# A SwiGLU feed-forward in split fp32 on one core: per-set pairs with an interleaved down projection, against shared weights and a down phase of its own

## Chip, cores and metric

One core of one Trainium2 chip. The metric is the device time of one execution of the whole kernel in microseconds (us); the median of three runs stands for a kernel. The profile of one further execution shows where the time goes. Engines: PE is TensorE's matmul unit (PEld its weight load), DVE is VectorE, ACT is ScalarE, POOL is GpSimd, SP is SyncE, which here issues the DMAs.

## What is computed

One layer of an encoder for T = 1088 tokens (1024 prompt and 64 sample tokens), width 1024, inner width 2816. The part at issue comes last: the output projection of the mixing branches, a norm, and the gated feed-forward.

```python
x = x + mixed @ w_out
h = rmsnorm(x, g_ffn)
return x + (jax.nn.silu(h @ w_gate) * (h @ w_up)) @ w_down
```

## The kernel before

All tensors are float32, and TensorE is given each operand as a rounded high part and a remainder: a product of two blocks is three matmuls, high by high, high by low, low by high (`matmul3`, L115). A high part is made by a copy with rounding (ACT, or POOL in `round_hi`, L91), a remainder by a subtraction on DVE (`lo_of`, L85). "Preparing" a block below means these two steps. Weights come in blocks of 512 KB through a ring of three tiles `raw` (or two tiles `fr`) in SBUF; `wblock` (L102) loads and prepares one.

Activations lie with the channels on the partitions and the tokens along the free axis. The tokens are two sets, `SETS`: set 0 is columns 0 to 511, set 1 columns 512 to 1087 (576 columns).

`y` (from L960) holds the residual stream in SBUF from here to the end. `out_proj(i)` (L1005) adds `mixed @ w_out` for set i, block row f by block row f, and sums the squares; `norm_stat` and `norm_rows` turn these into `rb`, a row of norm factors on all partitions. `block_sums(i, rb)` (L1053) multiplies the norm in and forms, for the four channel blocks k, the seven block combinations of the activations that a product by seven multiplications of 2x2 blocks needs, each with its high part (`hi`) and remainder (`lo`). For set 0 it runs inside `out_proj(1)`, whose matmuls cover it. For set 1 its 28 combinations are called at one place, between the last pair of set 0 and the first of set 1 (L1193).

The feed-forward (driver from L1176) goes over sets, and in a set over 11 pairs p of inner blocks. `hidden(p, i)` (L1137) makes gate and up, each by `pair_product` (L1092): seven products of a weight combination (`ws`, four or five of them by an add on POOL or DVE, prepared into `ah` and `al`) with the activation combinations, 12 matmuls each of 256 columns (set 0) or 288 (set 1). The results leave PSUM one by one, four by ACT copies to `st`, and are put together by adds on POOL and DVE. So each weight combination is made and prepared twice, once per set: 2 x 11 x 14 = 308 times. The hidden values u = silu(gate) * up stay in SBUF, prepared.

`down(p, us, i)` (L1156) is cut into eight units (one for each block row of the output), which are put between the products of the next pair: six matmuls and a DVE add of the result to `y` (L1170), 264 adds in all. After the last pair each finished block of `y` goes out at once (L1172).

What sets the order: the program is written as above, a scheduler then gives each engine one fixed order; an instruction waits for its data, for a free buffer of its ring, and for everything ahead of it on its engine. SP issues all DMAs in such an order too, so that a DMA that waits holds those behind it.

## Time and profile before

| | us |
|---|---|
| runs, median (lowest to highest) | 1814.99 (1814.76 to 1815.98) |
| the profiled execution | 1814.24 |
| its span | 1812.5 |
| PE busy | 1745.9 (96%), 12066 matmuls |
| DVE busy | 1437.3 (79%), 2767 instructions |
| ACT busy | 842.1 (46%) |
| POOL busy | 832.7 (46%) |
| DMA moved | 198.25 MB, mean 109 GB/s, fullest fortieth of the span 256 GB/s |
| chain of waits that ended last: share of PE | 60% |

The time of a run is the span and some 1.7 us around it. "Busy" counts an instruction from its start to its modelled end, and matmuls overlap, so that a busy PE still has its pace: what a matmul costs is the distance from its start to the next one's. The granted clock says how fast TensorE was allowed to run; at half of it every matmul takes twice as long.

### The profile page before, as it was taken

The numbers are of one execution on the slowest core, as the hardware profiler recorded it, in microseconds if no ns is written. First come the engines' busy times: TensorE is split into PE (matmuls) and PEld (weight loads), VectorE is DVE, ScalarE is ACT, GpSimd is POOL, SyncE is SP. The second block draws the span as 40 slices with busy tenths as digits, with TensorE's granted clock in tenths as the row PEclk, the third lists the DMA queues.
The fourth block names the chain that finished last, engine by engine and source line by source line (L and its number), as shares of the span: only waits on it lengthen the run. The fifth ranks groups of instructions, "written<-read, shape, count | busy, mean of one in ns | idle before, by whom it ended". The sixth has DMA issues, their size and how long they took to land.

```text
span 1812.5 us, 32877 instructions
## 1 busy us (share of the span) xinstructions
PE 1745.9 (96%) x12066; PEld 1679.2 (93%) x12066; DVE 1437.3 (79%) x2767; ACT 842.1 (46%) x1977; POOL 832.7 (46%) x885
## 2 busy tenths in 40 slices
PE   6999999999999998999999899999997899999999
PEld 6999999899999997899998889899996799999999
DVE  6657999998853436877664899899899999898896
ACT  4456677736423443477422443444443434344442
POOL 4102323343531125876014666566657665555543
PEclk9999999999999998999999999999998899999999
DMA  7223431134365327620543223232232232222322
GB/s 226 64 66 94 160 119 57 65 114 129 105 182 150 99 91 256 199 81 12 223 133 93 82 82 105 84 123 86 96 103 82 99 111 93 83 92 84 105 76 71
DMA packets 123598, 198.25 MB, mean 109 GB/s; under 512 B 21031, under 2 KB 91807, under 8 KB 123438
## 3 DMA queue, kind: packets, MB, share of 16 engines
q1 hardware_dynamic: 123438, 196.16, 33.8%
q8 instruction: 95, 1.56, 0.4%
q14 instruction: 65, 0.53, 0.1%
HBM read 158.47 MB, written 37.65 MB: 108 GB/s over the span
## 4 chain that ended last, share of the span: by engine, by line
PE 60%; DVE 6%; POOL 4%; issue 2%; ACT 1%; DMA 1%; SPq 0%; DVEq 0%; ACTq 0%; POOLq 0%
PE mm L120 46%; PE fl L120 8%; PE acc L927 2%; DVE lo L86 1%; PE tr L892 1%; PE mm L916 1%; DVE al L86 1%; DMA side_a<-gt 1%; POOL sm L901 1%; POOL pr L902 1%; DVE wlo L86 1%; DVE ws L1109 0%; POOL ws L1109 0%; PE mm L600 0%; ACT pr L900 0%
## 5 line engine op out<-in xcount | busy, mean ns | idle before, releaser
L120 PE MATMUL mm<-hi,ah 128*128 128x256 f32 (+1 forms) x1232 | 357.8, 291 | 9.7 <-ACT hi L1080 6.1
L120 PE MATMUL mm<-hi,al 128*128 128x256 f32 (+1 forms) x1232 | 357.6, 291 | 7.7 <-DVE al L86 7.7
L120 PE MATMUL mm<-lo,ah 128*128 128x256 f32 (+1 forms) x1232 | 358.4, 291 | 5.6 <-DVE lo L86 5.6
L86 DVE TENSOR_TENSOR al<-ws,ah 128x512 fp32r<-128x512 f32 x220 | 218.3, 1004 | 54.6 <-ACT ah L1114 52.2
L120 PE MATMUL mm<-u,whi 128*128 128x288 f32 (+1 forms) x1056 | 258.2, 330 | 0.7 <-DVE u L86 0.7
L1114 ACT CAST ah<-ws 128x512 fp32r<-128x512 f32 x220 | 135.4, 619 | 248.9 <-POOL ws L1109 141.9
L120 PEld LDWEIGHTS mm<-hi,ah 128*128 128x128 f32 x1232 | 234.4, 190 | 17.0 <-ACT hi L1080 8.3
L120 PEld LDWEIGHTS mm<-lo,ah 128*128 128x128 f32 x1232 | 234.1, 190 | 11.3 <-DVE lo L86 6.9
L120 PEld LDWEIGHTS mm<-hi,al 128*128 128x128 f32 x1232 | 233.3, 190 | 12.0 <-DVE al L86 11.3
L120 PE MATMUL fl<-hh,whi 128*128 128x362 f32 (+1 forms) x576 | 189.7, 330 | 0.7 <-ACT hh L133 0.7
L120 PE MATMUL fl<-hl,whi 128*128 128x362 f32 (+1 forms) x576 | 190.3, 331 | 0.0
L120 PE MATMUL fl<-hh,wlo 128*128 128x362 f32 (+1 forms) x576 | 189.3, 329 | 0.0
L120 PEld LDWEIGHTS mm<-u,whi 128*128 128x128 f32 x1056 | 175.1, 189 | 9.3 <-DVE u L86 1.1
L120 PE MATMUL mm<-u,wlo 128*128 128x288 f32 (+1 forms) x528 | 174.0, 330 | 0.0
L1109 POOL TENSOR_TENSOR ws<-raw 128x512 f32<-128x512 f32 x66 | 88.5, 1353 | 116.7 <-DVE al L86 116.7
L1170 DVE TENSOR_TENSOR y<-mm,y 128x288 f32<-128x288 f32 (+1 forms) x264 | 134.6, 523 | 7.4 <-PE mm L120 7.4
L96 POOL TENSOR_SCALAR whi<-raw 128x1024 fp32r<-128x1024 f32 x44 | 55.2, 1255 | 182.1 <-PE mm L120 168.4
L120 PE MATMUL mm<-tmhi,hh 128*128 128x256 f32 (+3 forms) x432 | 122.8, 289 | 1.2 <-POOL tmhi L96 1.1
L120 PE MATMUL mm<-tmlo,hh 128*128 128x256 f32 (+3 forms) x432 | 122.3, 285 | 0.7 <-DVE tmlo L86 0.7
L120 PE MATMUL mm<-tmhi,hl 128*128 128x256 f32 (+3 forms) x432 | 122.2, 285 | 0.0
L762 ACT ACTIVATE junk_a<-score,cand_a,sgn_a 128x512 f16<-128x512 f32 (+2 forms) x93 | 95.5, 1027 | 46.4 <-DVE cand_a L779 22.7
L86 DVE TENSOR_TENSOR wlo<-raw,whi 128x1024 fp32r<-128x1024 f32 x76 | 103.6, 1363 | 13.1 <-ACT whi L94 7.1
(369 smaller groups left out, 4865.4 us busy)
## 6 DMA issues: line engine op xcount, KB each, us to landing
raw<-in_w_up_dram SPq DMA_DIRECT2D x44, 512.0 KB, 4.1
fr<-in_w_gate_dram SPq DMA_DIRECT2D x44, 512.0 KB, 4.4
raw<-in_w_down_dram SPq DMA_DIRECT2D x44, 512.0 KB, 4.6
fraw<-in_w_gates_dram SPq DMA_DIRECT2D x24, 512.0 KB, 3.8
side<-side_a SPq DMA_DIRECT2D x8, 1088.0 KB, 6.9
raw<-in_w_out_dram SPq DMA_DIRECT2D x16, 512.0 KB, 3.6
gt<-side_m SPq DMA_DIRECT2D x16, 384.0 KB, 4.6
raw<-in_w_om_dram SPq DMA_DIRECT2D x12, 512.0 KB, 4.4
```

The costliest lines, as they stand in the source:

```text
L86: V.tensor_tensor(lo, src, hi.bitcast(F32), op=OP.subtract)
L96: G.tensor_scalar(hi, src, 1.0, 1.0, op0=OP.mult, op1=OP.mult)
L120: PE.matmul(ps, l, r, start=i == 0, stop=i == n - 1)
L762: A.activation(junk[:n, :nk], sc, AF.Sign, bias=bj, scale=1.0 if scale is None else scale[:n, j:j + 1], accum_out=sj)
L892: PE.matmul(lg[:n, i * 512:i * 512 + cn], qT[:, h, :n], kT[:, kv, s, k0 + c:k0 + c + cn], start=s == 0, stop=s == 1)
L901: G.tensor_tensor(sm, sm, mone[:n], op=OP.pow)
L902: G.tensor_scalar(pr, pr, sm, 0.5, op0=OP.mult, op1=OP.mult)
L916: PE.transpose(pt[:cn, i * n:(i + 1) * n], probs[i][:, c:c + cn], ident[:n, :n])
L927: PE.matmul(acc, l, r[:, es], start=ji == 0 and par == 0 and i == 0, stop=ji == nj - 1 and par == 1 and i == 2)
L1109: (V if m in (0, 5) else G).tensor_tensor(t, w, part(*z), op=op)
L1114: A.copy(wf, w)
L1170: V.tensor_tensor(y[:, f, c0:c0 + cn], ps, y[:, f, c0:c0 + cn], op=OP.add)
```

## The change

`y` is split in two tiles, one for each set, and `out_proj` also writes each finished block to DRAM (`y_d`), so that both tiles are given up once the norms are in. The seven products are put in another form, in which results that are summed share a PSUM bank: `chain` takes four products, `side` two, `one` one, and three intermediate sums leave by ACT copies while DVE makes three adds (before: four copies, POOL adds and four DVE adds). Of the four weight combinations three are made on DVE and one on POOL.

The first three pairs (`EARLY`) run for set 0 alone. The combinations of set 1 (`second_sums`, the new `block_sums(1, k, ...)` in four pieces) are called after pair 0 (piece 0), pair 1 (pieces 1 and 2) and pair 2 (piece 3). Pairs 0 to 2 follow for set 1, and pairs 3 to 10 for both sets with one preparation of the weights: 196 in place of 308. u is not prepared but stored to DRAM (`u_d`).

Down is a phase of its own. For each of three column chunks (364, 362, 362 columns, `CH`) the whole result, 8 blocks, stands in the 8 PSUM banks, while 22 inner blocks kb go by: u is loaded back (`uf`) and prepared (`uh`, `ul`), a weight block of 512 KB is loaded and prepared, 24 matmuls follow. At a chunk's end each block is added to its part of `y_d` (ring `yt` of three tiles) and stored. The host lays `w_down` out by kb, and the loads become 66 of rows of 4 KB (before 44). `round_hi` uses ACT alone from the first pair on (`third[0] = 2`).

```diff
-        if turn[0] % 2 and third[0]:
+        if third[0] and (turn[0] % 2 or third[0] > 1):
             A.copy(hi, src)
...
+ys = [None, yp.tile([128, KT, SETS[1][1]], F32, name="y1")]
+y_d = dram.tile([KT, 128, T], F32, name="y_d")
...
-                V.tensor_tensor(y[:, f, c0:c1], ps, y[:, f, c0:c1], op=OP.add)
+                V.tensor_tensor(y[:, f, d0:d1], ps, y[:, f, d0:d1], op=OP.add)
+                SP.dma_start(y_d[f, :, c0:c1], y[:, f, d0:d1])
...
+    def block_sums(i, k, rb, H, sums):
...
+        for e in range(2):
+            kk = k + 4 * e
+            V.scalar_tensor_tensor(hb[e][:, :n], ys[i][:, kk], gffn_c[:, kk:kk + 1], rb[:, :n], op0=OP.mult, op1=OP.mult)
+        b11, b12, b21, b22 = hb[0][:, :h], hb[0][:, h:n], hb[1][:, :h], hb[1][:, h:n]
+        t1, t2, t3, t4 = [t[:, :h] for t in sums]
+        for q, x, z, op, y_ in ((0, b11, None, None, None), (4, t1, b12, OP.subtract, b11), (2, b22, None, None, None),
+                                (5, t2, b22, OP.subtract, t1), (6, t3, b22, OP.subtract, b12),
+                                (1, b21, None, None, None), (3, t4, b21, OP.subtract, t2)):
+            if op:
+                (G if q == 6 else V).tensor_tensor(x, z, y_, op=op)
+            A.copy(H[0][q][:, k], x)
+            lo_of(H[1][q][:, k], x, H[0][q][:, k])
...
+        def product(dst, w, q, start, stop, then):
+            if turn2[0] % 2 == 0:
+                pair_w[:] = split_tiles()
...
+            A.copy(wh, w)
+            lo_of(wlo, w, wh)
...
+            for i in sets:
+                j = 0
+                for k in range(4):
+                    x, z = HH[i][0][q][:, k], HH[i][1][q][:, k]
+                    for l, r in ((wh[:, k], x), (wh[:, k], z), (wlo[:, k], x)):
+                        PE.matmul(dst[i], l, r, start=start and j == 0, stop=stop and j == 11, skip_group_check=True)
+                        j += 1
+                then(i)
...
+        product(chain, a11, 0, True, False, lambda i: A.copy(t11[i], chain[i]))
+        s1 = wsum(V, a21, OP.add, a22)
+        product(side, s1, 4, True, False, lambda i: A.copy(t22[i], side[i]))
+        s2 = wsum(V, s1, OP.subtract, a11)
+        product(chain, s2, 5, False, False, lambda i: A.copy(t12[i], chain[i]))
+        s4 = wsum(V, a12, OP.subtract, s2)
+        product(side, s4, 2, False, True, add(t12, side))
+        s3 = wsum(G, a11, OP.subtract, a21)
+        product(chain, s3, 6, False, False, add(t22, chain))
+        product(one, a12, 1, True, True, add(t11, one))
+        product(chain, a22, 3, False, True, lambda i: finish(i, t21[i], chain[i]))
...
+            SP.dma_start(u_d[p][0, :, t0:t0 + n], gi[:, 0].rearrange("p c t -> p (c t)"))
...
+    EARLY = 3
+    for p in range(EARLY):
+        hidden(p, (0,), True)
+        if p == 0:
+            rb = norm_rows(1, *st.pop())
+        for k in ((0,), (1, 2), (3,))[p]:
+            second_sums(k, rb)
...
+    for p in range(EARLY):
+        hidden(p, (1,))
+    for p in range(EARLY, NP):
+        hidden(p, (0, 1))
...
+    for c0, cn in CH:
+        acc = [mm()[:, :cn] for f in range(KT)]
+        for kb in range(NF):
+            p, e = kb // 2, kb % 2
+            uf = dn.tile([128, 364], F32, name="uf", tag="uf", bufs=2)[:, :cn]
+            SP.dma_start(uf, u_d[p][e, :, c0:c0 + cn])
+            wh, wlo = wblock(a["w_down"][kb], (KT, 128))
+            uh, ul = [dn.tile([128, 364], F32R, name=nm, tag=nm, bufs=2)[:, :cn] for nm in ("uh", "ul")]
+            A.copy(uh, uf)
+            lo_of(ul, uf, uh)
+            for f in range(KT):
+                for j, (l, r) in enumerate(((wh[:, f], uh), (wh[:, f], ul), (wlo[:, f], uh))):
+                    PE.matmul(acc[f], l, r, start=kb == 0 and j == 0, stop=kb == NF - 1 and j == 2)
+        for f in range(KT):
+            yt = dn.tile([128, 364], F32, name="yt", tag="yt", bufs=3)[:, :cn]
+            SP.dma_start(yt, y_d[f, :, c0:c0 + cn])
+            V.tensor_tensor(yt, acc[f], yt, op=OP.add)
+            SP.dma_start(o[0][f, :, c0:c0 + cn], yt)
```

How the order moves, at three places (each row: line of its kernel, operation, output, inputs, shape; numbers tell buffers apart).

**The combinations of set 1 on DVE.** Before, at the turn from set 0 to set 1 (`tg` from L1070 are the normed channels, `lo` the remainders of the combinations):

```order
L1070 SCALAR_TENSOR_TENSOR tg_16726<-y_11018,gffn_c_336,rb_13648 128x576 x2
L86 TENSOR_TENSOR lo5_16678<-st_16704,hi5_16671 128x288
L1070 SCALAR_TENSOR_TENSOR tg_16749<-y_11018,gffn_c_336,rb_13648 128x576 x2
L1170 TENSOR_TENSOR y_11018<-mm_16886,y_11018 128x512
L86 TENSOR_TENSOR lo0_16673<-tg_16726,hi0_16666 128x288
L1078 TENSOR_TENSOR st_16727<-tg_16726 128x288
L86 TENSOR_TENSOR lo1_16674<-tg_16726,hi1_16667 128x288
L86 TENSOR_TENSOR lo2_16675<-st_16727,hi2_16668 128x288
L86 TENSOR_TENSOR lo0_16673<-tg_16749,hi0_16666 128x288
L1078 TENSOR_TENSOR st_16750<-tg_16749 128x288
```
Now, after pair 0 of set 0 (`fr` from L1073 are the normed channels; `wlo` and `ws` are the weights of pair 1, `tg0` its results):

```order
L1073 SCALAR_TENSOR_TENSOR fr_13230<-y1_11018,gffn_c_336,rb_12911 128x576
L1097 TENSOR_TENSOR ws_13098<-raw_13078 128x512
L86 TENSOR_TENSOR wlo_13057<-raw_12947,whi_13056 128x512
L1128 TENSOR_TENSOR tg0_12944<-mm_12950,tg0_12944 128x256
L86 TENSOR_TENSOR wlo_13057<-raw_13076,whi_13056 128x512
L1080 TENSOR_TENSOR st_13206<-fr_13208,st_13206 128x288
L86 TENSOR_TENSOR lo4_12643<-st_13206,hi4_12636 128x288
L86 TENSOR_TENSOR lo6_12645<-st_13206,hi6_12638 128x288
L86 TENSOR_TENSOR lo5_12644<-st_13206,hi5_12637 128x288
L86 TENSOR_TENSOR lo0_12639<-fr_13230,hi0_12632 128x288
L1097 TENSOR_TENSOR ws_13117<-ws_13098,raw_13076 128x512
L86 TENSOR_TENSOR wlo_13101<-ws_13098,whi_13100 128x512
```
The work has moved from the turn between the two sets to a place among the weights and the results of set 0's early pairs. All four pieces stand between the results of pair 0 and the end of pair 2's gate in DVE's order.

**SP at the end of a chunk.** Before, at the kernel's end:

```order
L1097 DMA raw_21373<-in_w_up_dram 128x1024
L1097 DMA raw_21375<-in_w_up_dram 128x1024
L110 DMA raw_21452<-in_w_down_dram 128x4x256
L110 DMA raw_21613<-in_w_down_dram 128x4x256
L110 DMA raw_21691<-in_w_down_dram 128x4x256
L1172 DMA out_0_dram<-y_11018 128x288 x16
```
Now, from the last weight loads of the first chunk into the second (`raw` and `uf` belong to the second chunk, `yt` and `out` to the first):

```order
L1222 DMA uf_18871<-u0_11645 128x362
L110 DMA raw_18945<-in_w_down_dram 128x1024
L1222 DMA uf_18907<-u1_11646 128x362
L1234 DMA out_0_dram<-yt_18795 128x364
L1234 DMA out_0_dram<-yt_18799 128x364
L1234 DMA out_0_dram<-yt_18803 128x364
L1232 DMA yt_18807<-y_d_11019 128x364
L110 DMA raw_18981<-in_w_down_dram 128x1024
L1232 DMA yt_18811<-y_d_11019 128x364
L1232 DMA yt_18815<-y_d_11019 128x364
L1222 DMA uf_18943<-u1_11646 128x362
```
The finished blocks now share SP's order with the next chunk's loads, and from the fourth block on a `yt` load stands behind the store that frees its tile.

**PE at the same place.** Before, units of the last pair (one PSUM tile for each block row):

```order
L120 MATMUL mm_21733<-u_21557,whi_21692 128x288 x2
L120 MATMUL mm_21733<-u_21557,wlo_21693 128x288
L120 MATMUL mm_21733<-u_21561,whi_21692 128x288 x2
L120 MATMUL mm_21733<-u_21561,wlo_21693 128x288
L120 MATMUL mm_21742<-u_21557,whi_21692 128x288 x2
```
Now, the first blocks kb of the second chunk (`mm_18827` to `mm_18834` are its eight banks; `uh_18843` is kb 0, `uh_18879` kb 1):

```order
L1229 MATMUL mm_18827<-uh_18879,wlo_18875 128x362
L1229 MATMUL mm_18828<-ul_18880,whi_18874 128x362
L1229 MATMUL mm_18828<-uh_18879,wlo_18875 128x362
L1229 MATMUL mm_18829<-ul_18880,whi_18874 128x362
L1229 MATMUL mm_18829<-uh_18879,wlo_18875 128x362
L1229 MATMUL mm_18830<-uh_18843,whi_18838 128x362
L1229 MATMUL mm_18830<-ul_18844,whi_18838 128x362
L1229 MATMUL mm_18830<-uh_18843,wlo_18839 128x362
L1229 MATMUL mm_18830<-uh_18879,whi_18874 128x362
L1229 MATMUL mm_18830<-ul_18880,whi_18874 128x362
L1229 MATMUL mm_18830<-uh_18879,wlo_18875 128x362
L1229 MATMUL mm_18831<-uh_18843,whi_18838 128x362
```
The first two blocks kb go through three banks, then both through the fourth bank, both through the fifth, and so on to the eighth; each of these banks is still the first chunk's until its block has been added on DVE.

## Rows read from the trace of the kernel before

**Rows 1.** The windows view, five stretches of the last part; columns in its second row, PEclk granted clock.

```profile
core 0: us, PE busy (x) PEld busy (x) DVE busy (x) ACT busy (x) POOL busy (x), PEclk, DMA share, GB/s
986.00:1040.00 54.00, 48.49 (x339) 47.56 (x337) 43.47 (x65) 19.44 (x47) 34.82 (x33) 0.94 0.29 84
1040.00:1076.00 36.00, 32.77 (x238) 30.82 (x239) 32.90 (x39) 18.61 (x38) 27.47 (x22) 0.95 0.24 80
1076.00:1366.00 290.00, 287.87 (x1980) 265.34 (x1978) 265.84 (x371) 121.74 (x236) 174.76 (x137) 1.00 0.30 99
1366.00:1421.00 55.00, 38.34 (x190) 31.14 (x190) 51.67 (x69) 22.91 (x51) 43.26 (x37) 0.78 0.20 64
1421.00:1809.00 388.00, 387.86 (x2897) 386.04 (x2895) 340.03 (x528) 153.40 (x280) 201.37 (x162) 1.00 0.28 93
```

**Rows 2.** Timeline of PE, four stretches; columns: start us, us, engine line operation.

```profile
174.72 0.33 PE L120 MATMUL fl<-hl,whi 128*128 128x364 f32 x1
...
178.39 0.33 PE L120 MATMUL fl<-hh,wlo 128*128 128x364 f32 x1
...
1150.28 0.28 PE L120 MATMUL mm<-lo,ah 128*128 128x256 f32 x1
...
1152.18 0.28 PE L120 MATMUL mm<-hi,al 128*128 128x256 f32 x1
...
1418.13 1.06 PE L120 MATMUL mm<-u,whi 128*128 128x512 f32 x2
1418.99 0.63 PE L120 MATMUL mm<-u,wlo 128*128 128x512 f32 x1
...
1424.94 0.62 PE L120 MATMUL mm<-u,whi 128*128 128x512 f32 x2
...
1426.33 0.29 PE L120 MATMUL mm<-hi,al 128*128 128x288 f32 x1
...
1429.12 0.29 PE L120 MATMUL mm<-hi,al 128*128 128x288 f32 x1
```

**Rows 3.** Timeline, first gate matmul and the end of the execution.

```profile
1040.07 0.39 PE L120 MATMUL mm<-hi,ah 128*128 128x256 f32 x1 [1.66 <-ACT ah L1114]
...
1808.56 0.29 PE L120 MATMUL mm<-u,wlo 128*128 128x288 f32 x1
...
1808.90 0.46 DVE L1170 TENSOR_TENSOR y<-mm,y 128x288 f32<-128x288 f32 x1 [0.34 <-PE mm L120]
```

**Rows 4.** PE's waits from 1370 to 1421, the longest group: us in total, times, longest.

```profile
PE mm L120 <- ACT hi L1080: 6.1, 5, 2.6
```

**Rows 5.** Timeline of DVE from 1400 to 1418.

```profile
1403.54 1.53 DVE L1070 SCALAR_TENSOR_TENSOR tg<-y,gffn_c,rb 128x576 f32<-128x576 f32 x2
...
1409.11 0.45 DVE L86 TENSOR_TENSOR lo<-tg,hi 128x288 fp32r<-128x288 f32 x1
1409.48 1.05 DVE L1078 TENSOR_TENSOR st<-tg 128x288 f32<-128x288 f32 x1
1410.46 1.04 DVE L86 TENSOR_TENSOR lo<-tg,hi 128x288 fp32r<-128x288 f32 x1
...
1417.37 0.68 DVE L86 TENSOR_TENSOR al<-ws,ah 128x512 fp32r<-128x512 f32 x1
```

**Rows 6.** Groups by line and shape, 1040 to 1810; x count, busy us, mean ns.

```profile
L86 DVE TENSOR_TENSOR wlo<-raw,whi 128x1024 fp32r<-128x1024 f32 x43 | 62.8, 1461 | 2.7 <-ACT whi L94 2.0 <-POOL whi L96 0.6
...
L94 ACT CAST whi<-raw 128x1024 fp32r<-128x1024 f32 x21 | 22.1, 1053 | 2.5 <-PE mm L120 2.5
...
L1078 POOL TENSOR_TENSOR st<-tg 128x288 f32<-128x288 f32 x12 | 15.0, 1271 | 5.4 <-DVE tg L1070 5.4
```

**Rows 7.** DMA issues: x count, KB each, median us from issue to landing.

```profile
raw<-in_w_down_dram SPq DMA_DIRECT2D x43, 512.0 KB, 4.6
...
out_dram<-y SPq DMA_DIRECT2D x16, 144.0 KB, 1.8
...
fpt<-gate_b SPq DMA_DIRECT2D x16, 181.0 KB, 2.7
```

More of the change, by code (lines that the diff above doesn't have):

```diff
@@ L1088, in encoder_step, with combos @@
-    PRODUCTS = ((0, (1, 0), OP.add, (1, 1)), (2, (0, 0), OP.add, (1, 1)), (3, (1, 1), None, None),
-                (5, (0, 0), None, None), (4, (0, 1), OP.subtract, (1, 1)), (1, (0, 0), OP.add, (0, 1)),
-                (6, (1, 0), OP.subtract, (0, 0)))
-    def pair_product(name, p, i, H, out, units, q0):
-        h = SETS[i][1] // 2
+    def combos(pool, i):
+        h = SETS[i][1] // 2
+        return [[pool.tile([128, 4, h], F32R, name=f"{nm}{q}") for q in range(7)] for nm in ("hi", "lo")]
@@ new lines, in block_sums @@
+    def block_sums(i, k, rb, H, sums):
+        n = SETS[i][1]
+        h = n // 2
+        hb = [fa.tile([128, 1024], F32, name="fr", tag="fr", bufs=2) for e in range(2)]
+        for e in range(2):
[10 more added lines that the diff above has]
+            lo_of(H[1][q][:, k], x, H[0][q][:, k])
@@ L1094, in pair_product @@
+    def pair_product(name, p, sets, outs, finish, early):
         raws = []
         for e in range(2):
-            raw = fa.tile([128, 1024], F32, name="fr", tag="fr", bufs=2) if name == "w_gate" else raw_tile()
+            raw = fa.tile([128, 1024], F32, name="fr", tag="fr", bufs=2) if name == "w_gate" and not early else raw_tile()
             SP.dma_start(raw.rearrange("p (k j) -> p k j", k=KT), a[name][p + e * NP])
             raws.append(raw)
-        def part(e, c):
-            return raws[e][:, c * 512:(c + 1) * 512]
@@ L1156, in down @@
[L1156 to L1174 removed]
+        a11, a12 = raws[0][:, :512], raws[0][:, 512:]
@@ new lines, in banks, with add @@
+        def banks():
+            return {i: mm()[:, :SETS[i][1] // 2] for i in sets}
+        t11 = {i: outs[i][:, 0, 0] for i in sets}
+        t12 = {i: outs[i][:, 0, 1] for i in sets}
+        t21 = {i: outs[i][:, 1, 0] for i in sets}
+        t22 = {i: outs[i][:, 1, 1] for i in sets}
+        chain, side, one = banks(), banks(), banks()
+        def add(t, ps):
+            return lambda i: V.tensor_tensor(t[i], ps[i], t[i], op=OP.add)
+        product(chain, a11, 0, True, False, lambda i: A.copy(t11[i], chain[i]))
@@ L1176, in encoder_step, with first_sums @@
+    turn2, pair_w = [0], []
+    u_d = [dram.tile([2, 128, T], F32, name=f"u{p}") for p in range(NP)]
     sq0 = out_proj(0)
     mix_c[1].__exit__(None, None, None)
-    hp = ctx.enter_context(tc.tile_pool(name="h2", bufs=1))
-    fa = ctx.enter_context(tc.tile_pool(name="fa", bufs=1))
-    H = []
+    hp0_c = tc.tile_pool(name="h0", bufs=1)
+    HH = [combos(hp0_c.__enter__(), 0)]
+    fa_c = tc.tile_pool(name="fa", bufs=1)
+    fa = fa_c.__enter__()
+    def first_sums():
+        rb = norm_rows(0, *st.pop())
+        for k in range(4):
+            sums = [fa.tile([128, 512], F32, name="ws", tag="ws", bufs=4) for _ in range(2)]
+            block_sums(0, k, rb, HH[0], [t[:, e * 256:e * 256 + 256] for t in sums for e in range(2)])
@@ L1181, in encoder_step @@
     st = []
-    sq1 = out_proj(1, {1: lambda: st.append(norm_stat(0, sq0)), 2: lambda: H.append(block_sums(0, norm_rows(0, *st.pop())))})
+    sq1 = out_proj(1, {1: lambda: st.append(norm_stat(0, sq0)), 2: first_sums})
+    st.append(norm_stat(1, sq1))
+    y0_c.__exit__(None, None, None)
     mix_c[0].__exit__(None, None, None)
-    fu = ctx.enter_context(tc.tile_pool(name="fu", bufs=1, side="right"))
-    units = []
-    for i in range(2):
-        for p in range(NP):
-            now, later = (units, []) if p < NP - 1 else (units[:5], units[5:])
-            us = hidden(p, i, H[i], now)
-            units = now + later
-            if i == 0 and p == NP - 1:
-                H.append(block_sums(1, rb))
-            while units:
-                units.pop(0)()
-            if i == 0 and p == 1:
-                st.append(norm_stat(1, sq1))
-            if i == 0 and p == 2:
-                rb = norm_rows(1, *st.pop())
-            units = down(p, us, i)
@@ L1201, in encoder_step, with second_sums @@
-    while units:
-        units.pop(0)()
+    hp1_c = tc.tile_pool(name="h1", bufs=1)
+    HH.append(combos(hp1_c.__enter__(), 1))
+    third[0] = 2
+    fu_c = tc.tile_pool(name="fu0", bufs=1, side="right")
+    fu = fu_c.__enter__()
+    def second_sums(k, rb):
+        sums = fu.tile([128, 4, 288], F32, name="st", tag="st", bufs=1)
+        block_sums(1, k, rb, HH[1], [sums[:, e] for e in range(4)])
+    EARLY = 3
[5 more added lines that the diff above has]
+            second_sums(k, rb)
@@ L1205 @@
+    for c in (fu_c, dn_c, hp1_c, fa_c, hp0_c):
+        c.__exit__(None, None, None)
 _OUTS = [(1, 1024, 1024), (1, 64, 1024), (1, 1, 1024, 2, 64), (1, 1, 1024, 2, 64), (1, 1, 1024, 32), (1, 1, 15, 512),
```

160 lines of the change are left out of this document (50 added, 110 removed).

## Prediction

> **What bounds the kernel now.** I began with the page's first two parts: PE is busy 96% of the span, and no other engine has over 80%. So I asked what PE's matmuls need at their full pace, and where more time went. In the timeline [rows 2] the distance between two starts is the pace: 16 distances of 256 columns in 1.90 us are 0.119 each, 21 of 288 columns 0.133, 6 of 512 columns 0.232, 22 of 364 columns 0.167.
>
> Gate and up are 1848 matmuls of 256 and 1848 of 288 columns (2 x 11 x 7 x 12 each), 465.5 us. Down is 528 of 512 and 1056 of 288, 262.6 us. Together 728.1 us. The feed-forward lasts from 1040.07 to the last matmul at 1808.56 [rows 3], 768.6 us with that one. So 40.5 us are lost in it, and the windows [rows 1] show where. From 1421 on nothing is lost. From 1366 to 1421, where the combinations of set 1 are made, PE is idle for 16.7 us, and the clock of 0.78 takes 0.22 x 38.3 = 8.4 more: 25.1. From 1040 to 1076 it is 3.2 + 0.05 x 32.8 = 4.9. By subtraction some 10 are left for 1076 to 1366, in stalls that the overlap of matmuls mostly hides from the busy column. In out_proj(1), 986 to 1040, 5.5 + 0.06 x 48.5 = 8.4 are lost. In all 49 us before the last matmul can be won; DVE is what PE waits for in most of these places.
>
> **The change, part by part.** The number of gate and up matmuls and their columns stay, so I count what is lost after against these 49.
>
> *Shared preparation.* 112 preparations go, each an ACT cast, a DVE remainder and mostly a sum. In pairs 3 to 10 PE has 7 x 12 x (0.119 + 0.133) = 21.2 us for seven products, DVE 7 remainders, 3 sums and 6 adds, under 10. But DVE was not the bound from 1421 on: 388 us there lost nothing with DVE at 88% [rows 1]. So the saving is worth only the 10 us of 1076 to 1366. I leave 1 in the shared pairs, and 4 in set 1's pairs 0 to 2 (range 1 to 8), where the weight ring of two tiles comes free late at each gate's start.
>
> *out_proj(1) and the first pair.* Before, 8.4 + 4.9 = 13.3 were lost. POOL now makes one combination in place of four, DVE two more, 3 us over the stretch on an engine at 43.5 of 54. The 24 stores of y lie on SP between loads that are early. I take half, 7, with 3 and 14 as bounds.
>
> *Combinations of set 1.* In DVE's order of the changed kernel all four pieces stand between the results of pair 0 and the gate of pair 2. DVE's own cost is the distance of starts: the 128x288 remainder at 1409.11 is followed 0.37 later though 0.45 long, so 0.08 come off each duration [rows 5]. A piece has two multiplications of 0.73, seven remainders and three sums of 0.37: 5.2; four pieces 20.7. In the same stretch, from the first row that reads the norms to the last remainder of pair 2's up, stand 28 remainders and 15 sums of 128x512 at 0.60, 25.8, and 13 adds from PSUM (no more than 0.38, by the 288-column add in [rows 3]), four multiplications and two remainders of 364 columns, 7.5 together. That is 54 us on DVE. PE has 29 products of 12 matmuls there, 41.4 us. The difference, 12.6, PE must wait, and half-clock time and ring waits come on top: raw has three tiles for four weight blocks of a pair, I take 2. POOL makes about nine sums beside them. Beside POOL the same remainder took 1.04 in place of 0.45 [rows 5], so nine collisions cost 5.4. Sum 20, where 25.1 were lost before; bounds 12 (no collision, no ring wait) and 32 (also the clock down as in 1366 to 1421).
>
> The Trainium skill (SBUF — State Buffer, "Who interferes with whom") calls the port pair that VectorE shares with GpSimd an exclusive lock, and an instruction that meets it is fully blocked. The trace agrees only in part: the POOL operation there lasts 1.27 on average [rows 6], and the remainder grew by 0.59, not by 1.27. By the rule nine collisions would cost up to 11 and the sum would rise by 6.
>
> *Down.* 1584 matmuls of 364 or 362 columns at 0.167 are 264.2, against 262.6: +1.6. Each kb gives PE 4.0 us. Its weight chain, ACT 1.05 then DVE 1.46 [rows 6] and some 0.5 each for u, is under 4. The load of 512 + 182 KB in 4.0 us is 177 GB/s; the page's fullest slice moved 256. So I keep PE as the bound, and 1 us for the start.
>
> *Two chunk boundaries.* All eight banks are held until each block is added, and the ring yt has three tiles. From the fourth block on a tile goes round: store landed (1.8), load landed (2.7) [rows 7], add (0.5): 5.0 a turn. Blocks 0 to 2 are added within about 1 us of the last matmul, since kb 0's remainders stand ahead on DVE; the fourth then 5 after, the seventh and eighth 10 and 10.5 after. PE can do the matmuls of kb 0 and 1 meanwhile, 8.0 us, in its order the eighth block's six last, and kb 2 begins at about 12. SP also holds the weight load of kb 4 between the yt loads, 1 more. So 5 are lost. After waits of up to 2.6 us [rows 4] the clock fell before, and 512 columns took 0.43 in place of 0.232 [rows 2]; I add 2.5. Two boundaries: 15, bounds 8 (loads land in 1.9, clock holds) and 26.
>
> *The end.* Before, 3.9 us lie between the last matmul and the span's end [rows 3]. Now the last chunk's blocks take two turns of the ring of 5.0, from about 1.5 ahead of the end of the matmuls, then an add and a store, 2.7: 11.4. That is +7.5.
>
> **Sum.** Lost after: 7 + 20 + 4 + 1 + 1.6 + 1 + 15 = 49.6, against 49: +0.6. With the end +8.1 on the profiled execution's 1814.24: 1822.3, and 1823 for the median, which lies 0.75 higher. What the shared weights and the spread combinations win, the three serial chunk ends give back.
>
> **Rivals.**
> 1. *The early pairs cover the combinations.* If the norms of set 1 are ready some 10 us earlier than I read from the order, so that DVE starts the pieces while PE still has most of pair 0's up ahead, the two engines meet at the end and the 20 become 7 (2 for the ring, 5 for collisions). For it: the pairs by themselves leave DVE free, at 16 of PE's 20 us each. Against it: the place of the first piece in DVE's order, behind pair 0's last remainders. The point from which it decides is 42 us of DVE work after the norms. Alone it gives 1823 - 13 = 1810; with boundaries at 5 each, 1805. This is the faster side, chance 0.25.
> 2. *Boundaries worse than reckoned.* If kb 2 and kb 3 wait as well, because u and weights stand behind yt in SP's order, and the clock falls at each boundary so that 48 matmuls take 16 us and not 8, each costs 13: 1823 + 11 = 1834. With the early stretch at its bound of 32 it is 1846. Chance 0.15. The Trainium skill (TensorE: Matmul & The Clock Gate, "HAM oscillation — how this bites in real kernels") says that a kernel whose waits for data lie between short bursts of matmuls begins each burst at the low clock. The clock of 0.78 in 1366 to 1421 agrees.
> 3. *Down is bound by loads.* If 694 KB cannot come every 4.0 us, and the rate is the 105 to 109 GB/s that this kernel averages, a kb takes 6.6 and the phase 66 x 2.6 = 170 longer: 1990. Against it stands the slice of 256 GB/s. Chance 0.03.
> 4. *The change moves nothing that matters*: DVE was covered anyway, combinations and boundaries end where the old losses were, 1811 to 1818. This is the forecast's lower end; I give it 0.17 of its own.
>
> **Numbers.** A measurement of this kernel can tell 0.2%, 3.6 us, from no change. The forecast (1819 to 1832) has 0.40. Faster by more, under 1811.4: rival 1, 0.25, and a little of rival 4, 0.02. Within: the rest of rival 4, 0.15. Slower: the rest, 0.58. The range from 1805 to 1842 leaves out rival 3, the worst of rival 2, and the edge of rival 1. The forecast's own range with its near bounds is 1816 to 1835.
>
> **What would show it.** Right: PE's pace in pairs 3 to 10 without loss; PE's waits in the early pairs on DVE's remainders wlo and on sums, some 20 us, with DVE full; at two places of the down phase PE at half its work for about 12 us, waiting for DVE's yt adds, which wait for DMA; 11 us between the last matmul and the end. Wrong: PE waits on uf or raw all through down; DVE has idle time in the early stretch while PE waits there; or the boundaries pass in 8 us.

## The result and the profile after

The changed kernel takes 1830.60 us (median of 4 runs, 1828.46 to 1832.30), the kernel before 1815.22 beside it (4 runs, 1814.76 to 1815.98): a ratio of 1.0085, 95% interval 1.0069 to 1.0101. It is slower, by 15.4 us where 8 were forecast. The profiled execution took 1828.46, its span 1826.7, 14.2 more than before.

The timeline of PE gives the three stretches that the prediction counted. First the kernel before (its first matmul of 288 columns in out_proj(1); its other marks stand in [rows 3]):

```profile
977.82 0.29 PE L120 MATMUL mm<-xh,whi 128*128 128x288 f32 x1
```

Then the changed kernel: the same matmul, the first of a gate, the last of all, and the last row of its DVE timeline with the add of a block:

```profile
976.10 0.29 PE L120 MATMUL mm<-xh,whi 128*128 128x288 f32 x1
...
1033.76 0.36 PE L1114 MATMUL mm<-hi,whi 128*128 128x256 f32 x1
...
1814.34 0.33 PE L1229 MATMUL mm<-uh,wlo 128*128 128x362 f32 x1
...
1822.64 1.06 DVE L1233 TENSOR_TENSOR yt<-mm,yt 128x362 f32<-128x362 f32 x2 [3.12 <-DMA yt<-y_d]
```

| us | before | after | change |
|---|---|---|---|
| start of out_proj(1) (unchanged work ahead of it) | 977.8 | 976.1 | -1.7 |
| out_proj(1), 384 matmuls need 51.0 | 62.2 | 57.7 | -4.6 |
| feed-forward, first gate to last matmul | 768.6 | 780.8 | +12.1 |
| of it needed at PE's pace | 728.1 | 729.7 | +1.6 |
| of it lost | 40.5 | 51.0 | +10.5 |
| last matmul to the span's end | 3.8 | 12.2 | +8.4 |

The windows view of the changed kernel shows where the 51 us are (columns as in [rows 1]):

```profile
1036.00:1056.00 20.00, 18.64 (x156) 18.33 (x154) 13.38 (x25) 11.04 (x23) 3.16 (x3) 1.00 0.32 95
1056.00:1076.00 20.00, 13.68 (x89) 12.36 (x88) 19.16 (x36) 10.70 (x26) 4.30 (x4) 0.91 0.19 65
1076.00:1100.00 24.00, 16.94 (x106) 15.91 (x106) 22.45 (x46) 12.33 (x29) 6.36 (x3) 0.86 0.41 129
1100.00:1130.00 30.00, 26.19 (x189) 24.91 (x190) 23.66 (x43) 14.06 (x30) 6.26 (x3) 0.94 0.45 138
1130.00:1200.00 70.00, 68.35 (x512) 67.64 (x511) 49.72 (x85) 33.53 (x68) 8.35 (x5) 1.00 0.34 115
1200.00:1545.00 345.00, 345.00 (x2716) 345.00 (x2715) 165.56 (x300) 122.39 (x256) 25.11 (x15) 1.00 0.23 78
1545.00:1622.00 77.00, 77.00 (x467) 77.00 (x466) 33.13 (x41) 28.04 (x39) 0.00 (x0) 1.00 0.57 180
1622.00:1640.00 18.00, 13.27 (x58) 11.12 (x57) 6.78 (x10) 3.65 (x6) 0.00 (x0) 0.81 0.75 234
```

Where 25 us were lost before, with set 1's combinations made at one place, nothing is lost now: from 1200 to 1622, the shared pairs and the first chunk of down, PE is full, with DVE at about half (165.56 of 345) where it had 88%. The loss has moved. Among the early pairs, from 1056 to 1100, PE makes 195 matmuls in 44 us, 23 us of work at 0.119, while DVE is busy for 41.6 of the 44; and the granted clock is down after the waits, to means of 0.91 and 0.86. At each chunk boundary PE stands and slows down again (row 1622 to 1640). PE's waits in both places (us in total, times, longest), first 1036 to 1130, then the boundaries:

```profile
PE mm L1114 <- ACT whi L1106: 8.8, 6, 3.0
PE mm L1114 <- DVE wlo L86: 4.2, 4, 2.2
PE mm L1114 <- DVE tu L1128: 2.3, 1, 2.3
...
PE mm L1229 <- DVE yt L1233: 7.6, 6, 2.2
PE mm L1229 <- ACT uh L1225: 1.7, 2, 0.9
```

The longest group of the early pairs, PE behind ACT's casts of the weights, leads back in good part to DVE: the largest of ACT's own waits there (1056 to 1130) is for weight sums that stand in DVE's order. The next, 8.6 us, is for PE itself.

```profile
ACT whi L1106 <- DVE ws L1097: 9.0, 8, 2.5
```

The boundary in PE's timeline: the first matmuls of kb 0 and of kb 2, for the second and the third chunk.

```profile
1621.38 0.33 PE L1229 MATMUL mm<-uh,whi 128*128 128x362 f32 x1
...
1637.98 0.77 PE L1229 MATMUL mm<-uh,whi 128*128 128x362 f32 x3 [0.86 <-ACT uh L1225]
...
1717.58 0.33 PE L1229 MATMUL mm<-uh,whi 128*128 128x362 f32 x1
...
1734.90 1.60 PE L1229 MATMUL mm<-uh,whi 128*128 128x362 f32 x8 [0.87 <-ACT uh L1225]
```

16.6 and 17.3 us for 48 matmuls that need 8.0: 8.6 and 9.3 lost. At the starts of set 1's three pairs 2.5 are lost, 0.84 each, where PE waits for DVE's adds (waits from 1130 to 1200):

```profile
PE mm L1114 <- DVE tu L1128: 1.6, 3, 0.6
```

So 31 of the 51 are left for the early pairs. The timeline of DVE and SP at the first boundary shows the ring's turns:

```profile
1620.12 1.42 DVE L1233 TENSOR_TENSOR yt<-mm,yt 128x364 f32<-128x364 f32 x3
...
1620.68 1.39 SPq L1234 DMA_DIRECT2D out_dram<-yt  x3
...
1624.65 0.33 SPq L1232 DMA_DIRECT2D yt<-y_d  x1
...
1627.11 0.54 DVE L1233 TENSOR_TENSOR yt<-mm,yt 128x364 f32<-128x364 f32 x1 [2.94 <-DMA yt<-y_d]
1627.67 3.61 SPq L1234 DMA_DIRECT2D out_dram<-yt  x3
...
1631.38 1.84 SPq L1232 DMA_DIRECT2D yt<-y_d  x3
...
1633.93 0.54 DVE L1233 TENSOR_TENSOR yt<-mm,yt 128x364 f32<-128x364 f32 x1 [3.01 <-DMA yt<-y_d]
```

Three adds, three stores, a load 4 us after the store's issue, when that store has landed, the next add 2.5 us after that. From the first add to the fourth are 7.0 us, from the fourth to the seventh 6.8.

### The profile page after: what moved, and what is told of

The parts are those of the page before. It is cut to its first block, busy times and chain, and to the rows that moved or that the text cites. A ratio compares the mean times of both kernels' runs of the same rounds, so it can differ in the third digit from the quotient of the medians.

```text
span 1826.7 us, 32204 instructions
## 1 busy us (share of the span) xinstructions
PE 1744.2 (95%) x12066; PEld 1703.0 (93%) x12066; DVE 1155.4 (63%) x2457; ACT 820.6 (45%) x1931; POOL 431.9 (24%) x551
## 4 chain that ended last, share of the span: by engine, by line
PE 61%; DVE 5%; DMA 3%; POOL 2%; issue 1%; ACT 1%; SPq 0%; DVEq 0%; POOLq 0%; ACTq 0%
PE mm L1114 24%; PE mm L1229 13%; PE mm L120 10%; PE fl L120 8%; PE acc L927 2%; PE tr L892 1%; PE mm L916 1%; DMA yt<-y_d 1%; DVE lo L86 1%; DVE wlo L86 1%; DMA out_dram<-yt 1%; POOL sm L901 1%; DMA side_a<-gt 1%; POOL pr L902 1%; DMA raw<-in_w_up_dram 1%
## 5 line engine op out<-in xcount | busy, mean ns | idle before, releaser
L1114 PE MATMUL mm<-hi,whi 128*128 128x256 f32 (+1 forms) x1232 | 359.1, 292 | 15.9 <-ACT whi L1106 8.8
L1114 PE MATMUL mm<-hi,wlo 128*128 128x256 f32 (+1 forms) x1232 | 357.1, 293 | 4.3 <-DVE wlo L86 4.2
L1114 PE MATMUL mm<-lo,whi 128*128 128x256 f32 (+1 forms) x1232 | 357.9, 291 | 0.0
L86 DVE TENSOR_TENSOR wlo<-raw,whi 128x1024 fp32r<-128x1024 f32 (+1 forms) x149 | 155.1, 1049 | 185.1 <-ACT whi L94 141.1
L1114 PEld LDWEIGHTS mm<-hi,whi 128*128 128x128 f32 x1232 | 236.2, 192 | 19.3 <-ACT whi L1106 10.3
L1114 PEld LDWEIGHTS mm<-hi,wlo 128*128 128x128 f32 x1232 | 235.0, 192 | 5.5 <-DVE wlo L86 5.5
L1114 PEld LDWEIGHTS mm<-lo,whi 128*128 128x128 f32 x1232 | 236.3, 192 | 0.0
L1229 PE MATMUL mm<-ul,whi 128*128 128x362 f32 (+1 forms) x528 | 175.2, 332 | 1.1 <-DVE ul L86 1.1
L1229 PE MATMUL mm<-uh,wlo 128*128 128x362 f32 (+1 forms) x528 | 175.0, 333 | 0.0
L120 PEld LDWEIGHTS fl<-hh,whi 128*128 128x128 f32 x576 | 108.5, 189 | 1.7 <-issue 1.1
```

Source lines behind the costliest of these rows:

```text
L86: V.tensor_tensor(lo, src, hi.bitcast(F32), op=OP.subtract)
L120: PE.matmul(ps, l, r, start=i == 0, stop=i == n - 1)
L1114: PE.matmul(dst[i], l, r, start=start and j == 0, stop=stop and j == 11, skip_group_check=True)
L1229: PE.matmul(acc[f], l, r, start=kb == 0 and j == 0, stop=kb == NF - 1 and j == 2)
```

## The experiments

All times are medians; each run stands beside the kernel before on the same chip (1814.25 to 1815.01), and the ratio is to that. Differences between two runs are differences of their medians.

**1. Eight tiles for the blocks of y.** Part of the change is relieved: the ring that makes the chunk ends serial.

```diff
+    fu_c.__exit__(None, None, None)
+    yq_c = tc.tile_pool(name="yq", bufs=1, side="right")
+    yq = yq_c.__enter__()
     for c0, cn in CH:
...
-            yt = dn.tile([128, 364], F32, name="yt", tag="yt", bufs=3)[:, :cn]
+            yt = yq.tile([128, 364], F32, name="yt", tag="yt", bufs=8)[:, :cn]
```

> The ring yt gets eight tiles, in the room that the hidden phase's tiles leave, so that a chunk's eight blocks of y can be loaded before its last matmul and no load waits for a store. Theory (the ring's round trips of store, load and add make the boundary stalls of 8.1 and 9.5 us and the long end): about 2 us stay at each boundary (eight adds of 0.45 in a row, and kb 1's remainder behind them), and the end falls from 11.7 to about 5: 13 + 6 less, near 1812. Rival (the banks and the clock, not the ring, make the stall): at most 6 less, from the end alone, near 1825.

Measured: 1807.07, ratio 0.9951 (0.9937 to 0.9966): 23.5 less than the change and faster than the kernel before. In DVE's timeline all eight adds now follow each other:

```profile
1620.71 3.64 DVE L1236 TENSOR_TENSOR yt<-mm,yt 128x364 f32<-128x364 f32 x8
```

and PE's waits over both boundaries (1600 to 1740) are down to one:

```profile
PE mm L1232 <- ACT uh L1228: 0.4, 1, 0.4
```

The last matmul starts at 1797.79 and the span ends at 1803.0, so that the end has 5. From 1622 to 1640 PE is now full, at a granted clock of 1.00. (The stalls that the expectation puts at 8.1 and 9.5, and the end at 11.7, are 8.6, 9.3 and 12.2 by the lines above.) The ring made both boundary stalls, even the 2 us each that I left for adds, and the long end. The clock drop there went with them: a consequence, not a cause of its own.

**2. The pieces tied to the pairs, five early pairs.**

```diff
+            if early and nm == "tu":
+                return fu.tile([128, 1152], F32, name="tu0", tag="tu0", bufs=bufs)[:, :4 * h].rearrange("p (e c t) -> p e c t", e=2, c=2)
...
-        sums = fu.tile([128, 4, 288], F32, name="st", tag="st", bufs=1)
+        sums = fu.tile([128, 1152], F32, name="tu0", tag="tu0", bufs=1)
...
-    EARLY = 3
+    EARLY = 5
...
-        for k in ((0,), (1, 2), (3,))[p]:
+        for k in ((0,), (1,), (2,), (3,), ())[p]:
```

> The pieces of the set-1 combinations are tied to the pairs: their sums use the one buffer of the pairs' up result, so that piece k can start only when pair k's results are gone and must end before pair k+1's up begins. Five pairs are early in place of three. Theory (DVE is full with 54 us of work against 41 of PE's because the pieces are bunched): DVE has 16 + 5 us for each pair against PE's 20, the loss of about 29 us between 1046 and 1130 falls to about 10, and two pairs more with weights prepared twice cost about 2: near 1814. Rival (late weights, four blocks of a pair through a ring of three, make the loss): no gain, 1829 to 1834.

Measured: 1838.20, ratio 1.0124 (1.0108 to 1.0140), 7.6 more than the change. Neither came true. Three windows of 26 us, each of about one early pair (168 matmuls, 20 us of PE's work), are alike:

```profile
1054.00:1080.00 26.00, 21.20 (x162) 19.61 (x162) 23.27 (x43) 13.91 (x32) 4.91 (x3) 1.00 0.32 102
1080.00:1106.00 26.00, 22.05 (x168) 20.42 (x167) 22.25 (x41) 13.47 (x30) 4.54 (x3) 1.00 0.33 103
1106.00:1132.00 26.00, 21.81 (x166) 20.34 (x166) 22.62 (x42) 13.31 (x30) 4.18 (x3) 1.00 0.38 126
```

DVE idles for 3 of 26 us while PE waits for it: 22 us of DVE work for 20 of PE's would allow about 22, but a piece has to fit where the tie puts it, and some weights come late (DVE waits 3.6 us for loads of w_gate from 1050 to 1160). Which of the two matters more is not shown. And the run changes two things: five early pairs in place of three also mean two more pairs without sharing, which run 4 below prices at some 3 us each. So it does not show that the tie itself costs anything.

**3. Early gate weights in tiles of their own.**

```diff
-        hb = [fa.tile([128, 1024], F32, name="fr", tag="fr", bufs=2) for e in range(2)]
+        hb = [fu.tile([128, 576], F32, name="hb", tag="hb", bufs=2) if i else fa.tile([128, 1024], F32, name="fr", tag="fr", bufs=2) for e in range(2)]
...
-            raw = fa.tile([128, 1024], F32, name="fr", tag="fr", bufs=2) if name == "w_gate" and not early else raw_tile()
+            raw = fa.tile([128, 1024], F32, name="fr", tag="fr", bufs=2) if name == "w_gate" else raw_tile()
...
-            t = fa.tile([128, 512], F32, name="ws", tag="ws", bufs=4)
+            t = fa.tile([128, 512], F32, name="ws", tag="ws", bufs=3)
```

> Early pairs load their gate weights into the two tiles fr as the later pairs do, so that the ring of three serves the up weights alone; the normed channels of set 1 get two small tiles of their own, the ring of weight sums three tiles in place of four. The pieces stay bunched. Theory (DVE is full): the loss of 29 us falls by 2 to 5, what the waits on weight loads show: near 1827. Rival (late weights): the loss falls by 15 or more: 1815 or less.

Measured: 1823.87, ratio 1.0052 (1.0036 to 1.0068): 6.7 less, a little more than the theory's 2 to 5 and far from the rival's 15. Four weight blocks of a pair through three tiles cost about 7 us, where 2 had been put down for ring waits and half-clock time together. The size is rough, since the runs go from 1820.44 to 1828.25, and the edit also gives the normed channels tiles of their own.

**4. No sharing.** All pairs run for set 0, then all for set 1 (`EARLY = 11`, from the fourth pair on with the later pairs' weight tiles).

> All 11 pairs run for set 0 alone and then for set 1 alone, so that no weight preparation is shared; everything else stays. Theory (sharing is worth next to nothing on PE's path, since DVE fits beside it): about 0.8 us per additional set-1 pair at its gate's start, and as much for a set-0 pair, 5 to 12 in all: 1836 to 1842. Rival (sharing is what keeps PE fed): pairs wait for weights or DVE as in the early stretch, 30 or more: above 1860.

Measured: 1855.22, ratio 1.0218 (1.0203 to 1.0233), 24.6 more: between the two, above my bound of 12. PE's waits from 1150 to 1300, where set 0 runs alone:

```profile
PE mm L1114 <- DVE wlo L86: 8.3, 8, 1.2
```

and the windows of that stretch and of 1310 to 1545, where set 1 runs alone:

```profile
1150.00:1300.00 150.00, 139.98 (x1139) 137.14 (x1138) 121.39 (x194) 74.50 (x156) 23.38 (x14) 1.00 0.34 115
1310.00:1545.00 235.00, 229.49 (x1708) 227.13 (x1707) 172.15 (x294) 116.33 (x233) 33.41 (x20) 1.00 0.35 116
```

By matmuls and pace, 150 - 1139 x 0.119 = 14.5 us are lost in nearly seven set-0 pairs, some 2 each, 8.3 of them in waits for late remainders, and 235 - 1708 x 0.133 = 8 in ten set-1 pairs, 0.8 each, though DVE has 29 us of 150 free. Sharing is worth more in this form of the products than DVE's busy share says. Why a lone pair loses them was not tested; the weight ring of two double tiles is a guess. In all, 24.6 over eight more pairs without sharing is some 3 us a pair.

**5. The norms of set 1 earlier**, which is the condition of the prediction's first rival, with some 7 of its 10 us.

```diff
-        hidden(p, (0,), True)
-        if p == 0:
-            rb = norm_rows(1, *st.pop())
+        hidden(p, (0,), True, (lambda: rbs.append(norm_rows(1, *st.pop()))) if p == 0 else None)
```

> The norms of set 1 are made between gate and up of pair 0 in place of after pair 0, on PE some 7 us earlier; nothing else changes, and the pieces stay bunched. Theory (from the norms on DVE has more work than PE, and before them it has 6 us idle): DVE starts the pieces about 7 us earlier and the loss of the early pairs falls by 5 to 7: near 1824.5. Rival (the loss comes from late weights and the order of rows, not from DVE's start): 1829 to 1833.

Measured: 1831.06, ratio 1.0088 (1.0072 to 1.0105): no gain, the rival's time. The windows show why the theory's sum fails:

```profile
1046.00:1070.00 24.00, 17.33 (x122) 15.53 (x121) 23.94 (x45) 14.07 (x33) 3.75 (x4) 0.89 0.25 85
1070.00:1090.00 20.00, 16.12 (x96) 15.59 (x96) 18.55 (x38) 13.03 (x31) 6.39 (x3) 0.76 0.40 124
1090.00:1110.00 20.00, 17.55 (x120) 16.63 (x120) 14.83 (x28) 7.42 (x15) 1.71 (x1) 0.86 0.46 154
```

DVE starts the pieces earlier, is full from 1046 on, and PE waits from 1046 on; afterwards, 1090 to 1110, DVE has 5 us free and PE still loses time (120 matmuls, 14.3 us of 20), partly at half clock, partly because a load of w_gate went out on SP only at 1093.66 (DVE waits 1.2 us for it).

**6 and 7. Together.** Runs 1 and 3, and then 5 on top.

> The ring of eight tiles for y and the gate weights in fr, together. Their places are 500 us apart, so the gains should add: 1830.6 - 23.5 - 6.7 = 1800. If the second gain came from elsewhere (the chunk boundaries, where runs with three tiles differ by some us), 1805 to 1807.

Measured: 1798.43, ratio 0.9909 (0.9894 to 0.9924). The gains add, and the kernel is faster than the one before.

> As the run before, and the norms of set 1 between gate and up of pair 0. Theory: another 5 to 7 less: 1794. Rival: 1800.

Measured: 1799.76, ratio 0.9917 (0.9902 to 0.9932). Again no gain from earlier norms, here without late weights.

**8. Five tiles in the old place** (`bufs=5`).

> The ring yt in its old place with five tiles in place of three. Theory (turns of the ring of about 5 us each decide): the blocks 0 to 4 are added at once and 5 to 7 one turn later, about 5.5 after the chunk's last matmul, while PE has 8 us of work in kb 0 and 1. The boundaries lose 0 to 2 each, the end about 7 to 8: 1830.6 - 16 - 4 = 1811. Rival (SP's order, in which loads of the next chunk stand behind stores, makes the stalls): boundaries stay above 5 each, 1820 or more.

Measured: 1822.83, ratio 1.0039 (1.0026 to 1.0052), 7.8 less where I expected 20. DVE's timeline at the boundary:

```profile
1623.52 2.30 DVE L1233 TENSOR_TENSOR yt<-mm,yt 128x364 f32<-128x364 f32 x5
...
1632.61 0.54 DVE L1233 TENSOR_TENSOR yt<-mm,yt 128x364 f32<-128x364 f32 x1 [5.03 <-DMA yt<-y_d]
```

Blocks 0 to 4 go at once, as expected, but the turn takes 9.1 us and not 5. The stores of the first chunk (KB each, median us from issue to landing), of the change and then of this run:

```profile
out_dram<-yt SPq DMA_DIRECT2D x8, 182.0 KB, 2.8
```

```profile
out_dram<-yt SPq DMA_DIRECT2D x8, 182.0 KB, 5.4
```

Five stores in a row beside the next chunk's weights land later, and the loads of y at this place too (median 3.5 in place of 2.9, 1619 to 1640). The number of tiles and the length of a turn are not independent. The time is the one that the rival gave, and the boundaries still lose 6.3 and 6.4. Its cause, the place in SP's order, is not what SP shows at the first one: SP issues nothing from 1626.8 to 1629.0, and then the sixth block's load when the first store has landed, 4.9 us after that store's issue.

**9. The remainders of set 1 left out**, on the kernel of run 6.

```diff
+            if i:
+                A.copy(H[1][q][:, k], x)
+            else:
                 lo_of(H[1][q][:, k], x, H[0][q][:, k])
```

> On the kernel with the ring of eight and the gate weights in fr (1798.4). The 28 remainders of set 1's combinations are left out: ACT writes the high part there a second time, so the low-order part of the products of set 1 is not that of the reference. DVE loses 28 x 0.37 = 10.4 us of work between the norms and pair 2's gate. Theory (the amount of DVE's work in that stretch makes PE wait): 8 to 10 less, near 1789. Rival (not the amount but the place of the rows in the order and the rings of weights): less than 3, 1796 or more.

Measured: 1794.08, ratio 0.9885 (0.9868 to 0.9902): 4.3 less, between theory and rival. Windows of run 6, then of this run:

```profile
1054.00:1100.00 46.00, 39.25 (x294) 37.02 (x293) 45.04 (x84) 26.51 (x61) 6.48 (x6) 0.96 0.31 103
```

```profile
1054.00:1100.00 46.00, 39.95 (x300) 37.81 (x299) 43.70 (x74) 38.22 (x100) 12.28 (x7) 0.96 0.33 109
```

Ten fewer rows on DVE gave six more matmuls here. ACT took on 12 us, 38 of 46 now, so a part of the gain may be hidden behind it, which the run doesn't show.

**10 and 11. The pieces tied, with the weights in time**: run 6 with the tie of run 2 and five early pairs, then with a looser tie (the pieces' sums in a ring of three with the gate results, `EARLY = 4`, piece p after pair p).

> On the same kernel, the pieces tied one to each of the first four pairs, as in the second run, and five early pairs; now the weights don't share a ring of three. Theory (late weights undid the spreading in the second run; DVE has 21 us for PE's 20 in each pair): the early pairs lose about 9 in place of 20, two more unshared pairs cost 3: near 1790. Rival (a piece must fit into one gate, 13 us on DVE against 10 on PE): no gain, 1797 to 1801.

Measured: 1802.68, ratio 0.9931 (0.9916 to 0.9946), 4.3 more than run 6, a little more than the rival's 1797 to 1801.

> On the same kernel, the pieces share a ring of three with the pairs' gate results and four pairs are early: each piece may run from the end of the pair before until two pairs on, a looser tie than in the run before. Theory (the amount counts, and place matters if a piece stands ahead of weights that PE needs): 3 to 6 less from the wider window, 1 more for the additional pair: near 1795. Rival: 1798 to 1801.

Measured: 1796.97, ratio 0.9901 (0.9886 to 0.9917), 1.5 less than run 6, whose runs span 1796.38 to 1799.44: between theory and rival, not clearly better, and no worse with a further unshared pair. As in run 2, the runs 10 and 11 change the tie and the number of unshared pairs at once; the table after run 12 takes this up.

**12. Three sums of each piece on POOL**, on run 11.

```diff
-                (G if q == 6 else V).tensor_tensor(x, z, y_, op=op)
+                (G if q == 6 or i else V).tensor_tensor(x, z, y_, op=op)
```

> On the kernel of the run before, the three sums of each piece that DVE makes go to POOL as well, which is busy for only 4 of 20 us there. DVE loses 12 x 0.37 = 4.4 us of its work from the norms on. Theory (amount of DVE's work, with little contention): 2 to 3 less, 1794 to 1795. Rival (contention: beside a POOL sum a DVE row of two inputs grew by 0.3 to 1.1 us in the changed kernel, and there are 12 POOL sums more): 5 or more come on top, 1799 to 1803.

Measured: 1803.36, ratio 0.9940 (0.9923 to 0.9956), 6.4 more: the rival's time. Groups of DVE rows, 1050 to 1130, of run 11 and then of this run:

```profile
L86 DVE TENSOR_TENSOR wlo<-ws,whi 128x512 fp32r<-128x512 f32 x26 | 17.5, 689 | 0.3 <-ACT whi L1106 0.3
L86 DVE TENSOR_TENSOR lo<-hb,hi 128x288 fp32r<-128x288 f32 x12 | 5.2, 444 | 0.0
```

```profile
L86 DVE TENSOR_TENSOR wlo<-ws,whi 128x512 fp32r<-128x512 f32 x24 | 18.9, 811 | 2.1 <-ACT whi L1106 2.1
L86 DVE TENSOR_TENSOR lo<-hb,hi 128x288 fp32r<-128x288 f32 x12 | 7.7, 666 | 0.0
```

The mean of the same remainder rose from 444 to 666 ns. That this makes the loss is not shown: from 1046 to 1130 DVE was busy for 77.4 us here and for 80.6 in run 11, so that it had more time left and not less. ACT's casts waited 7.4 us for the sums, which are slower on POOL, and POOL's own weight sums from `raw` took 2.9 us on average in place of 1.6. How the 6.4 divide between these is open.

**The feed-forward alone.** The work ahead of out_proj(1) is the same in all these kernels, but in the profiled executions out_proj(1) starts anywhere from 975.8 (run 1) to 981.0 (run 8), which is more than some of the differences above. From the start of the first gate matmul to the start of the last matmul of all, the profiled executions took:

| run | us | unshared early pairs |
|---|---|---|
| the change | 780.6 | 3 |
| 2 (tie) | 785.7 | 5 |
| 4 (no sharing) | 805.9 | 11 |
| 6 | 754.7 | 3 |
| 7 (norms earlier) | 755.7 | 3 |
| 9 (remainders left out) | 748.9 | 3 |
| 10 (tie) | 756.5 | 5 |
| 11 (looser tie) | 751.8 | 4 |
| 12 (sums on POOL) | 758.0 | 4 |

By this measure run 9 gains 5.8 on run 6, run 11 gains 3.0, and run 10 loses 1.7. If a further unshared pair costs the 3 us of run 4, which is an estimate, the tie by itself gained some 4 us in run 10 and 6 in run 11. So bunching is probably a part of the loss; no run ties the pieces with three early pairs, which would show it.

## Why the prediction was right, and where it was off

The direction and the mechanism were right: what the combinations of set 1 no longer cost at their old place is given back in the early pairs, at two chunk boundaries and at the end. The size was off by a factor of nearly two, 8 against 15, by the terms below. That it was not off by more is in part luck. The early stretch, the boundaries and the end together were 15 us worse than put down, and some 8 came back elsewhere: out_proj(1) started 1.7 earlier, the old losses were 2.7 larger than the 49 counted (out_proj(1) as a whole had lost 11.2 and not 8.4), and set 1's pairs, the shared pairs and the start of down lost 3.5 less than put down.

- *Shared pairs and down*: right. 1 + 1 + 1.6 were put down; PE loses nothing from 1200 to 1622, nor in the two later chunks behind their first two blocks kb, and 1584 matmuls keep their 0.167. DMA carries 180 GB/s there (the row 1545 to 1622), so the third rival, down bound by loads, is out. The text that the saving "is worth only the 10 us" was read against the old kernel; run 4 shows that the new products without sharing would cost 24.6 more.
- *Set 1's pairs*: 4 put down, 2.5 measured. PE waited for DVE's adds `tu` there, not for the weight ring that the prediction named.
- *out_proj(1)*: 7 left for it and the first pair. out_proj alone lost 6.7 (57.7 against 51.0), so that the number is nearly used up by it; the first pair's loss is in the next term.
- *Combinations of set 1*: the step that failed most. "54 us on DVE" against "41.4" of PE, a difference of 12.6, 2 for rings, 5.4 for collisions: 20. Measured about 31. The 2 stood for ring waits and half-clock time together. The ring was worth 7 to 9 (run 3 against the change, run 6 against run 1). The clock took, by the windows, 0.09 x 13.7 + 0.14 x 16.9 + 0.06 x 26.2 = 5.2; the two overlap, since the clock falls after waits. That 2 is the term that was mis-sized for certain. Beside it, the difference of two totals seems not to be what PE waits. If it were, earlier norms (runs 5, 7) would have paid, since DVE had 6.6 of 20 us free from 1036 to 1056; and run 9 would have paid 8 to 10 for 10.4, where it paid 4.3 (5.8 in the feed-forward alone), with ACT busier. DVE goes through its rows in the fixed order, in which a piece stands ahead of weights that PE needs at once; PE stands for that, and when the pieces are done DVE has time left that wins nothing back: from 1100 to 1130 it idles for 6.3 us of 30 while PE stands for 3.8 at a clock of 0.94, one of the prediction's own signs of being wrong. How the 31 divide beyond the ring is not settled; by the estimate after run 12 some 4 to 6 of them may come from bunching.
- *Collisions*: five DVE rows of the stretch grew, by some 3.6 us in all where 5.4 were put down, but the way I read the one row of before was wrong. POOL's and DVE's timelines of the change at the first collision:

```profile
1056.47 1.71 POOL L1097 TENSOR_TENSOR ws<-raw 128x512 f32<-128x512 f32 x1
```

```profile
1056.98 1.52 DVE L1080 TENSOR_TENSOR st<-fr 128x288 f32<-128x288 f32 x1
1058.42 0.45 DVE L86 TENSOR_TENSOR lo<-fr,hi 128x288 fp32r<-128x288 f32 x1
```

POOL's sum ends at 1058.18, DVE's sum 0.32 later, about its own length alone. The other two large ones do the same (DVE ends 0.32 and 0.55 behind POOL). So DVE waits for the rest of POOL's row and then runs. The 0.59 of [rows 5] was such a rest: the remainder at 1410.46 ended at 1411.50, 0.32 behind this row of POOL in the kernel before.

```profile
1410.18 1.00 POOL L1078 TENSOR_TENSOR tg<-tg 128x288 f32<-128x288 f32 x1
```

The Trainium skill's rule (SBUF — State Buffer, "Who interferes with whom"), of which I said that the trace agrees only in part, fits these three rows. The cost of a collision to DVE is what is left of the POOL row, up to 1.1 us in these. POOL can also be the one that is held up: the row below took 3.79, where one of the same shape at 1055.71 took 0.80. DVE's rows beside it kept their lengths, and ACT's cast of its result waited 2.2 us. The prediction had no term for that.

```profile
1081.53 3.79 POOL L1080 TENSOR_TENSOR st<-fr 128x288 f32<-128x288 f32 x1 [7.84 <-DVE lo L86]
```

- *Chunk boundaries*: 15 put down, 8.6 + 9.3 = 17.9 measured. The order of events is the forecast one (three blocks about 1 us ahead of the boundary, the fourth and seventh a turn later each), but "5.0 a turn" was 7.0: the first store landed 4.0 after its issue, not 1.8, and SP issued the load at once. Run 1 shows that the ring is all of it. Of the 15, twice 2.5 were for the clock, and that was right, as shown below; the waits were 13 in place of 10.
- *The end*: 11.4 put down (its parts add to 11.2), 12.2 measured.

Rival 1 asked for norms some 10 us earlier. Counted from the first gate, run 5 starts the pieces 12.9 us on, the change 20.3, and it gains nothing. The time lies between the forecast and rival 2, by an early stretch near its upper bound of 32. The cause that rival 2 named did not come: at the first boundary kb 2 waited for the eighth block and then for its own preparation, and ACT's cast of its weights had waited 13.6 us for matmuls to give its tile free, not for a load; kb 3 lost 0.1.

At both boundaries the clock fell after waits of about 2 us for an add (2.2 at the first, 2.2 and 1.9 at the second): some 15 matmuls were 0.30 us apart in place of 0.167, the lower of the clock's two levels, at which they took 1.8 times as long. The windows from the first matmul of kb 0 to that of kb 2:

```profile
1621.38:1637.98 16.60, 11.87 (x49) 9.74 (x48) 4.92 (x9) 2.94 (x5) 0.00 (x0) 0.79 0.76 242
1717.58:1734.90 17.32, 11.59 (x50) 9.77 (x49) 4.87 (x9) 2.94 (x5) 0.00 (x0) 0.80 0.74 234
```

That is 0.21 x 11.9 + 0.20 x 11.6 = 4.8 us for the clock. Where the waits were taken away (run 1), the mean clock of the execution rose from 0.986 to 0.993. The section of the Trainium skill that the prediction names with rival 2 (TensorE: Matmul & The Clock Gate, "HAM oscillation — how this bites in real kernels") says that short bursts of matmuls with waits for data between them start at the low clock. The trace agrees, with 0.79 and 0.80 here and 1.00 where the waits are gone.

The fastest kernel that computes the same is that of run 11, 1796.97; run 6, at 1798.43, is the same within their spread. Both are 1% faster than the kernel before, and run 6 needs only two changes of buffers on top of the change, which by itself was slower.
